# mLSTM heads on one core: scores from stacked key and query parts, row picks over 128 rows, partition sums from split operands

## The chip, the cores and the metric

One of the eight cores of a Trainium2 chip runs the whole program. The metric is the device time in microseconds; the kernel before has a median of 2092.24 us over 3 runs (2091.16 to 2093.17).

## The reference, cut to what matters

A two-layer decoder trunk, 512 tokens of width 1024, in float32: feed-forward (`ffn0`), mLSTM mixer, `ffn1`, shared keys and values (`kv`), `ffn2`, sparse attention (`nsa`), `ffn3`. Each feed-forward block is `h += 0.5 * (silu(a) * b) @ w_out` with `a, b = split(rmsnorm(h) @ w_in)`. The mLSTM has 8 heads (keys and queries of 64, values of 128). Per head, with all times before `t` in one causal triangle:

```
log_i, log_f = gate projections;  b = cumsum(log_f)
D[t,s] = b[t] - b[s] + log_i[s]   (s <= t);   m[t] = max over s
W[t,s] = exp(D[t,s] - m[t]) * (q[t] . k[s]) / 8
num[t] = sum_s W[t,s] v[s];   den[t] = sum_s W[t,s]
h_out  = rmsnorm(num / max(|den|, exp(-m))) * gain * sigmoid(og)
```

## The kernel before, in words

Everything is kept transposed: features on the 128 partitions, the 512 tokens along the free dimension. A float32 product of full accuracy is made from three matmuls of the type float32r: each operand is split into a rounded part `hi` (ScalarE, L152 or L124) and a rest `lo` (VectorE, L153 or L125), and `mm3` (L145) adds `hi*hi + hi*lo + lo*hi` in PSUM. All matmuls go through `mm` (L142), so the profile puts them on L143; they are told apart by tile names.

Weights come through `load_weight` (L105): a DMA on the SP queue into `wraw` (2 buffers), a split into `whi` and `wlo` (3 buffers each), two weights ahead of use. A plain float32 operand is accepted by TensorE too; the profile then shows two matmul instructions for one in the code.

The mLSTM stage (`mlstm`, L312) runs in this order (L534 to L551):

- the gate projection `pg` (40 of 128 output rows; PSUM tag `mm`, which has two buffers), then the query projection of the first pair of heads; then `rstd_rows` (the row scale `r`) and `gates` (L347), a chain of some 20 VectorE operations on 8 rows, which ends in the running maximum. Its rows are transposed (`um`, L379) and split by `pair` (L331) into `nM`, a tile of 40 rows: the `hi` rows at 0 to 7, the `lo` rows at 32 to 39.
- `project_qk` (L386) and `project_v` (L404) of four heads (half 0). Queries and keys of two heads share a tile of 128 rows, 64 rows each, as `qkh` and `qkl`.
- `heads(0)` (L447), woven with the output-gate projection `og`, 1.5 steps of it for each step of the heads. Per head: the decay matrix `E` for the next head (`decay`, L432; a row pick `sel[:, h, :]` of 40 rows spreads row `h` of `nM` over all partitions: tile `pnm`); the scores `S` in four causal strips of 512, 384, 256 and 128 columns, each an `mm3` over the head's 64 rows (L459); the product with `E` on VectorE (L466), its split `Wh`, `Wl`; the sum over strips on GpSimd (L469); the product with the values (`pn`, L477), its copy `num` and square `sqn` on ScalarE; and two plain float32 matmuls into the 40 rows of `dm` (L484, L485), which sum `E` and `sqn` over the partitions. The stationary operand is a slice of `hot`, all zeros but one column, so that the sum lands in the head's row.
- projections of half 1, woven with `finish(0)` (L490): a copy of `dm`, transposes, a short VectorE chain, and per head a row pick of `cr` (L513), two elementwise steps and a split into `yhi`, `ylo`. Then `heads(1)` woven with the output projection `out0` at 0.4, `finish(1)` woven with the rest of it, and the output projection of half 1.

A scheduler under this code orders the instructions of each engine by readiness and the order of the code, so engines' orders differ a little from what is written. Each feed-forward stage opens a pool of its own (L260); its first tile, `home` (L262), has a size that depends on the stage, 384, 128, 256 and 448 bytes for stages 0 to 3, and the tiles `ft`, `fu`, `ghi` and `glo` lie behind it. The pools of `ffn2` and `ffn3` begin behind the tiles of `kv` (L561 to L566), whose sizes add up to 37,376 bytes, 73 times 512.

Of the kernel before, what the change touches and what calls it, by code (L numbers as in the profile page):

```python
# [9 lines left out]
F32 = mybir.dt.float32  # L10
F32R = mybir.dt.float32r
# [14 lines left out]
THIRDS = ((0, 8), (8, 15), (15, 22))  # L26
HOME = (0, 256, 384, 64)
H = 8
# [62 lines left out]
class Net:  # L91
# [164 lines left out]
    def ffn(self, i, r=None):  # L256
        nc, tc = self.nc, self.tc
        with ExitStack() as ctx:
            pp = ctx.enter_context(tc.tile_pool(name=f"fps{i}", bufs=6, space=PSUM, reuse_waits="tile"))
            gp = ctx.enter_context(tc.tile_pool(name=f"fg{i}", bufs=8, reuse_waits="tile"))  # L260

            nc.vector.memset(gp.tile([P, (HOME[i] - 128) % 512 // 4], F32, name="home", tag="home", bufs=1)[:, :1], 0.0)  # L262
            x, ssq = self.norm_in(G_FFN + i * KB, r is None, i == 0)
# [48 lines left out]
    def mlstm(self):  # L312
        nc, tc = self.nc, self.tc
        TT, STT, TS = nc.vector.tensor_tensor, nc.vector.scalar_tensor_tensor, nc.vector.tensor_scalar
        with ExitStack() as ctx:
# [7 lines left out]

            sel = mp.tile([40, H, P], F32R, name="sel")
            nc.gpsimd.tensor_copy(sel, self.cst[:40, C_SEL:C_SEL + H][:, :, None].to_broadcast([40, H, P]))

            hot = mp.tile([P, 80], F32, name="hot")
            nc.gpsimd.memset(hot, 0.0)
            nc.gpsimd.memset(hot[:, 39:40], 1.0)

            def pair(name, src):  # L331

                t = mp.tile([40, T], F32R, name=name, tag="rows", bufs=2)
                nc.gpsimd.memset(t.bitcast(F32), 0.0)
                nc.scalar.activation(t[:H], src, AF.Copy)
                TT(t[32:], src, t[:H].bitcast(F32), op=ALU.subtract)
                return t


            w = self.weight("m_gate")  # L340
            pg = ps_mm()
            for k in range(KB):
# [43 lines left out]
            def project_qk(half):  # L386
                for j in range(2):
                    for kind in range(2):
                        w = self.weight("m_qk", 4 * kind + 2 * half + j)
                        ps = ps_mm()  # L390
                        for k in range(KB):
                            self.mm3(ps, self.strip(w, k), x[k], k == 0, k == KB - 1)
                            yield
                        s = mp.tile([P, T], F32, name="qks", tag="tmp", bufs=3)
                        if kind == 0:
                            STT(s, ps, 0.125, r, op0=ALU.mult, op1=ALU.mult)
                        else:
                            TT(s, ps, r, op=ALU.mult)
                        hi = mp.tile([P, T], F32R, name="qkh", tag="qk", bufs=8)
                        lo = mp.tile([P, T], F32R, name="qkl", tag="qk", bufs=8)  # L400
                        self.split(s, hi, lo)
                        qk[kind, 2 * half + j] = (hi, lo)

# [28 lines left out]
            def decay(h):  # L432

                nm = ps_nm()
                self.mm(nm, sel[:, h, :], nM, True, True)
                E = mp.tile([P, 1280], F32, name="E", tag="big", bufs=BIG)
                dg = mp.tile([P, NTB, P], F32, name="dg", tag="tmp", bufs=3)
                for sb in range(NTB):
                    u = uc[:, sb, h:h + 1]
                    STT(dg[:, sb, :], nm[:, sb * P:(sb + 1) * P], u, self.cst[:, C_CAUST:C_CAUST + P], op0=ALU.add, op1=ALU.add)  # L440
                    if sb < NTB - 1:
                        nc.scalar.activation(E[:, SEG[sb] + P:SEG[sb] + T - sb * P], nm[:, (sb + 1) * P:], AF.Exp, bias=u)
                for sb in range(NTB):
                    nc.scalar.activation(E[:, SEG[sb]:SEG[sb] + P], dg[:, sb, :], AF.Exp)
                return E

            def heads(half):  # L447
                first = 4 * half
                E = decay(first)
                d = dm[half] = pp.tile([40, T], F32, name="dm", tag="dm", bufs=1)  # L450
                for h in range(first, first + 4):
                    base = 64 * (h % 2)
                    pick = lambda t, a, b: (t[0][base:base + 64, a:b], t[1][base:base + 64, a:b])
                    q, k = qk[0, h // 2], qk[1, h // 2]
                    S = [pp.tile([P, T], F32, name="S", tag="S", bufs=3) for _ in range(3)]
                    for sb in (0, 1, 3, 2):
                        bank, c0 = BANK[sb]
                        n = T - sb * P
                        self.mm3(S[bank][:, c0:c0 + n], pick(k, sb * P, sb * P + P), pick(q, sb * P, T), True, True)  # L459
                        yield  # L460
# [22 lines left out]
                    yield  # L483
                    self.mm(d, hot[:, 39 - h:79 - h], E[:, :T], h == first, False)  # L484
                    self.mm(d, hot[:, 7 - h:47 - h], sq, False, h == first + 3)  # L485
                    num[h] = n
# [3 lines left out]
            def finish(half):  # L490

                d = dm[half]
                s = mp.tile([40, T], F32, name="ds", tag="tmp", bufs=3)
                nc.scalar.copy(s, d)
                pt = ps_nm()[:, :160].rearrange("p (t c) -> p t c", t=NTB)
# [15 lines left out]
                for h in range(4 * half, 4 * half + 4):  # L511
                    pc = ps_nm()
                    self.mm(pc, sel[:, h, :], cr, True, True)  # L513
                    n = num[h]
# [554 lines left out]
```

## Time and profile before

| | us |
|---|---|
| median of 3 runs | 2092.24 |
| the profiled execution, its own time | 2092.58 |
| its span, first to last instruction | 2090.8 |
| TensorE busy in the span | 2058.5 (98%) |
| mean granted TensorE clock | 0.998 |

The span is 1.8 us shorter than the execution's own time, which is the start and the end of the program. The matmuls overlap in the trace: one of 512 columns shows 390 ns, but the next starts some 227 ns after it. So costs on TensorE are read from start to start. "Idle before" in brackets is the time in which an engine had nothing running, with what ended it.

### The profile page before, as it was taken

The numbers are of one execution on the slowest core, as the hardware profiler recorded it, in microseconds if no ns is written. First come the engines' busy times: TensorE is split into PE (matmuls) and PEld (weight loads), VectorE is DVE, ScalarE is ACT, GpSimd is POOL, SyncE is SP. The second block draws the span as 40 slices with busy tenths as digits, with TensorE's granted clock in tenths as the row PEclk, the third lists the DMA queues.
The fourth block names the chain that finished last, engine by engine and source line by source line (L and its number), as shares of the span: only waits on it lengthen the run. The fifth ranks groups of instructions, "written<-read, shape, count | busy, mean of one in ns | idle before, by whom it ended". The sixth has DMA issues, their size and how long they took to land.

```text
span 2090.8 us, 24459 instructions
## 1 busy us (share of the span) xinstructions
PE 2058.5 (98%) x9492; PEld 1663.3 (80%) x9492; DVE 1144.4 (55%) x2020; ACT 767.4 (37%) x1269; POOL 160.4 (8%) x174
## 2 busy tenths in 40 slices
PE   8999999999999999999999999999999999999999
PEld 6888888767668888888877888888778788888887
DVE  6434445754765434445666444445899985434443
ACT  5222233344543223224343322224667663222231
POOL 1000001001220000000101000001343310000000
PEclk9999999999999999999999999999999999999999
DMA  4323332212112332323324323332121112232232
GB/s 158 93 99 99 95 100 87 88 61 71 61 59 90 94 101 90 102 94 97 111 91 124 108 95 95 97 97 88 51 61 41 36 57 91 92 100 96 96 99 93
DMA packets 55188, 186.02 MB, mean 89 GB/s; under 512 B 6560, under 2 KB 7200, under 8 KB 55072
## 3 DMA queue, kind: packets, MB, share of 16 engines
q1 hardware_dynamic: 54112, 182.37, 27.4%
q8 instruction: 74, 1.21, 0.2%
q0 software_dynamic: 384, 1.05, 0.2%
q10 hardware_dynamic: 576, 1.05, 0.1%
q14 instruction: 42, 0.34, 0.1%
HBM read 177.10 MB, written 2.10 MB: 86 GB/s over the span
## 4 chain that ended last, share of the span: by engine, by line
PE 92%; DVE 5%; ACT 1%; issue 1%; POOL 0%; DMA 0%; SPq 0%; ACTq 0%; DVEq 0%; POOLq 0%
PE pmm L143 81%; PE S L143 3%; PE po L143 2%; PE vps L143 1%; PE pt L862 1%; PE paux L143 1%; PE dm L143 1%; DVE wlo L125 1%; PE pn L143 1%; DVE pr L828 1%; DVE ptl L153 0%; DVE qh L745 0%; DVE Wl L153 0%; ACT xhi L187 0%; PE pnm L143 0%
## 5 line engine op out<-in xcount | busy, mean ns | idle before, releaser
L124 ACT ACTIVATE whi<-wraw 128x1024 fp32r<-128x1024 f32 (+4 forms) x399 | 359.8, 916 | 1023.4 <-PE pmm L143 838.2
L143 PE MATMUL pmm<-xhi,whi 128*128 128x512 f32 (+1 forms) x1680 | 664.5, 396 | 10.8 <-ACT whi L124 8.5
L143 PE MATMUL pmm<-xhi,wlo 128*128 128x512 f32 (+1 forms) x1680 | 658.6, 392 | 0.0
L143 PE MATMUL pmm<-xlo,whi 128*128 128x512 f32 (+1 forms) x1680 | 658.4, 392 | 0.0
L125 DVE TENSOR_TENSOR wlo<-wraw,whi 128x1024 fp32r<-128x1024 f32 (+4 forms) x399 | 421.8, 1068 | 82.3 <-ACT whi L124 71.7
L143 PEld LDWEIGHTS pmm<-xhi,whi 128*128 128x128 f32 (+1 forms) x1680 | 316.0, 188 | 82.1 <-ACT whi L124 9.7
L143 PEld LDWEIGHTS pmm<-xhi,wlo 128*128 128x128 f32 (+1 forms) x1680 | 315.6, 188 | 67.7 <-DVE wlo L125 1.1
L143 PEld LDWEIGHTS pmm<-xlo,whi 128*128 128x128 f32 (+1 forms) x1680 | 316.0, 188 | 62.4
L143 PE MATMUL pmm<-ghi,whi 128*128 128x512 f32 x704 | 276.1, 392 | 0.0
L143 PE MATMUL pmm<-ghi,wlo 128*128 128x512 f32 x704 | 275.7, 392 | 0.0
L143 PE MATMUL pmm<-glo,whi 128*128 128x512 f32 x704 | 275.1, 391 | 0.0
L271 DVE TENSOR_TENSOR fu<-pmm,r 128x512 f32<-128x512 f32 x88 | 60.8, 691 | 260.6 <-PE pmm L143 260.4
L309 DVE SCALAR_TENSOR_TENSOR h<-pmm,h 128x512 f32<-128x512 f32 x96 | 66.3, 691 | 250.6 <-PE pmm L143 250.6
L269 DVE TENSOR_TENSOR ft<-pmm,r 128x512 f32<-128x512 f32 x88 | 60.8, 691 | 174.8 <-PE pmm L143 174.8
L143 PEld LDWEIGHTS pmm<-ghi,wlo 128*128 128x128 f32 x704 | 132.2, 188 | 29.4
L143 PEld LDWEIGHTS pmm<-glo,whi 128*128 128x128 f32 x704 | 132.2, 188 | 29.1
L143 PEld LDWEIGHTS pmm<-ghi,whi 128*128 128x128 f32 x704 | 132.3, 188 | 28.2
L198 POOL TENSOR_TENSOR ssq<-ssq,sq 128x512 f32<-128x512 f32 x18 | 27.3, 1518 | 1024.2 <-ACT sq L197 1024.2
L152 ACT ACTIVATE ghi<-ft 128x512 fp32r<-128x512 f32 x88 | 55.7, 632 | 72.6 <-DVE ft L272 72.6
L829 ACT ACTIVATE pr<-pr,nx 128x512 f32<-128x512 f32 (+3 forms) x128 | 70.7, 555 | 8.6 <-DVE pr L828 7.9
L153 DVE TENSOR_TENSOR glo<-ft,ghi 128x512 fp32r<-128x512 f32 x88 | 60.4, 686 | 14.7 <-ACT ghi L152 14.7
L828 DVE TENSOR_SCALAR_CACHE_REDUCE pr<-S,cn 128x512 f32<-128x512 f32 (+3 forms) x128 | 66.1, 537 | 2.7 <-PE S L143 2.5
(289 smaller groups left out, 2037.5 us busy)
## 6 DMA issues: line engine op xcount, KB each, us to landing
wraw<-in_ffn_in SPq DMA_DIRECT2D x176, 512.0 KB, 3.4
wraw<-in_ffn_out SPq DMA_DIRECT2D x64, 448.0 KB, 3.4
wraw<-in_ffn_out SPq DMA_DIRECT2D x32, 512.0 KB, 3.5
wraw<-in_m_qk SPq DMA_DIRECT2D x8, 512.0 KB, 3.4
wraw<-in_m_v SPq DMA_DIRECT2D x8, 512.0 KB, 3.4
wraw<-in_m_og SPq DMA_DIRECT2D x8, 512.0 KB, 3.4
wraw<-in_m_out SPq DMA_DIRECT2D x8, 512.0 KB, 3.4
wraw<-in_kv_t SPq DMA_DIRECT2D x8, 512.0 KB, 3.5
```

Of the source, the lines that this page charges most:

```text
L124: nc.scalar.activation(hi[:p, c], raw[:p, c], AF.Copy)
L125: nc.vector.tensor_tensor(lo[:p, c], raw[:p, c], hi[:p, c].bitcast(F32), op=ALU.subtract)
L143: self.nc.tensor.matmul(out, lhsT, rhs, start=start, stop=stop)
L152: self.nc.scalar.activation(hi, src, AF.Copy)
L153: self.nc.vector.tensor_tensor(lo, src, hi.bitcast(F32), op=ALU.subtract)
L198: (nc.gpsimd if b < 4 else nc.vector).tensor_tensor(t, t, sq, op=ALU.add)
L269: nc.vector.tensor_tensor(t, pa, r, op=ALU.mult)
L271: nc.vector.tensor_tensor(u, pb, r, op=ALU.mult)
L309: nc.vector.scalar_tensor_tensor(h, po[j], 0.5, h, op0=ALU.mult, op1=ALU.add)
L828: TS(s, S[:, i, :n], cc, None, op0=ALU.mult, op1=ALU.min, accum_out=nx[:, i:i + 1])
L829: nc.scalar.activation(s, s, AF.Exp, bias=nx[:, i:i + 1], scale=-1.0, accum_out=z[:, i:i + 1])
L862: nc.tensor.transpose(pt[:, col:col + P], pr[br][:, ROW[tb] + sb * P:ROW[tb] + sb * P + P], self.ident)
```

## The change

- **Scores.** The keys of a head become one tile of 128 rows, `hi` on 64 rows and `lo` on the other 64; the queries of a head become two tiles, `hi` and `lo`, each held on both halves, the second by a DMA inside SBUF on the SP queue. A strip is then two matmuls over 128 rows in place of three over 64. The splits are made per head (64 rows) and no longer per pair.
- **Row picks.** `nM` and `cr` have 128 rows, zeros outside the 16 used, and `sel` is one column for each head, broadcast to 128 columns. `sel` and `hot` are written by ScalarE in place of GpSimd.
- **Partition sums.** `dm` has 128 rows. `E` and the square are split into `hi` and `lo` (ScalarE and VectorE) in tiles of the pool `stat`, and each sum is two float32r matmuls with 128 stationary columns.
- `pg` moves from PSUM tag `mm` (2 buffers) to tag `S` (3 buffers).
- `home` has 384 bytes in every feed-forward stage.

```diff
-            nc.vector.memset(gp.tile([P, (HOME[i] - 128) % 512 // 4], F32, name="home", tag="home", bufs=1)[:, :1], 0.0)
+            nc.vector.memset(gp.tile([P, 96], F32, name="home", tag="home", bufs=1)[:, :1], 0.0)
...
-            sel = mp.tile([40, H, P], F32R, name="sel")
-            nc.gpsimd.tensor_copy(sel, self.cst[:40, C_SEL:C_SEL + H][:, :, None].to_broadcast([40, H, P]))
-
-            hot = mp.tile([P, 80], F32, name="hot")
-            nc.gpsimd.memset(hot, 0.0)
-            nc.gpsimd.memset(hot[:, 39:40], 1.0)
+            sel = mp.tile([P, H], F32R, name="sel")
+            nc.scalar.activation(sel, self.cst[:, C_SEL:C_SEL + H], AF.Copy)
+            pick = lambda h: sel[:, h:h + 1].to_broadcast([P, P])
+
+            hot = mp.tile([P, 168], F32R, name="hot")
+            nc.scalar.activation(hot, self.cst[:, C_ID:C_ID + 1].to_broadcast([P, 168]), AF.Copy, scale=0.0)
+            nc.scalar.activation(hot[:, 39:40], self.ones[:, :1], AF.Copy)
...
-                t = mp.tile([40, T], F32R, name=name, tag="rows", bufs=2)
+                t = mp.tile([P, T], F32R, name=name, tag="rows", bufs=2)
...
-            pg = ps_mm()
+            pg = pp.tile([P, T], F32, name="pg", tag="S", bufs=3)
...
-                        hi = mp.tile([P, T], F32R, name="qkh", tag="qk", bufs=8)
-                        lo = mp.tile([P, T], F32R, name="qkl", tag="qk", bufs=8)
-                        self.split(s, hi, lo)
-                        qk[kind, 2 * half + j] = (hi, lo)
+                        for e in range(2):
+                            a, b = slice(64 * e, 64 * e + 64), slice(64 - 64 * e, 128 - 64 * e)
+                            if kind == 0:
+                                hi, lo = (mp.tile([P, T], F32R, name=n, tag="q", bufs=8) for n in ("qh", "ql"))
+                                self.split(s[a], hi[a], lo[a])
+                                for t in (hi, lo):
+                                    nc.sync.dma_start(t[b].bitcast(F32), t[a].bitcast(F32))
+                                qk[0, 4 * half + 2 * j + e] = (hi, lo)
+                            else:
+                                t = mp.tile([P, T], F32R, name="kk", tag="k", bufs=4)
+                                self.split(s[a], t[a], t[b])
+                                qk[1, 4 * half + 2 * j + e] = t
...
-                self.mm(nm, sel[:, h, :], nM, True, True)
+                self.mm(nm, pick(h), nM, True, True)
...
-                d = dm[half] = pp.tile([40, T], F32, name="dm", tag="dm", bufs=1)
+                d = dm[half] = pp.tile([P, T], F32, name="dm", tag="dm", bufs=1)
+                def total(row, src, last, *tags):
+                    hi, lo = (self.sp.tile([P, T], F32R, name=n, tag=t, bufs=k) for n, (t, k) in zip(("th", "tl"), tags))
+                    self.split(src, hi, lo)
+                    for t in (hi, lo):
+                        self.mm(d, hot[:, 39 - row:167 - row], t, row == first and t is hi, last and t is lo)
...
-                        self.mm3(S[bank][:, c0:c0 + n], pick(k, sb * P, sb * P + P), pick(q, sb * P, T), True, True)
+                        for part in range(2):
+                            self.mm(S[bank][:, c0:c0 + n], k[:, sb * P:sb * P + P], q[part][:, sb * P:], part == 0, part == 1)
...
-                    self.mm(d, hot[:, 39 - h:79 - h], E[:, :T], h == first, False)
-                    self.mm(d, hot[:, 7 - h:47 - h], sq, False, h == first + 3)
+                    total(h, E[:, :T], False, ("ssq0", 1), ("ssq1", 1))
+                    total(32 + h, sq, h == first + 3, ("sq", 2), ("sq", 2))
```

## Rows read from the trace of the kernel before

**Rows 1.** The page, busy time of the engines: us, share of span, instructions.

```profile
PE 2058.5 (98%) x9492; PEld 1663.3 (80%) x9492; DVE 1144.4 (55%) x2020; ACT 767.4 (37%) x1269; POOL 160.4 (8%) x174
```

**Rows 2.** The page, the chain that ended last, by line.

```profile
PE pmm L143 81%; PE S L143 3%; PE po L143 2%; PE vps L143 1%; PE pt L862 1%; PE paux L143 1%; PE dm L143 1%; DVE wlo L125 1%; PE pn L143 1%; DVE pr L828 1%; DVE ptl L153 0%; DVE qh L745 0%; DVE Wl L153 0%; ACT xhi L187 0%; PE pnm L143 0%
```

**Rows 3.** Windows of the mLSTM: us, then each engine's busy us (instructions), PEclk.

```profile
378.00:405.40 27.40, 25.12 (x110) 20.70 (x110) 21.84 (x42) 8.43 (x14) 0.00 (x0) 0.94 0.17 58
...
428.00:506.00 78.00, 76.92 (x311) 50.83 (x310) 39.18 (x66) 31.37 (x69) 10.47 (x12) 1.00 0.17 55
...
553.00:596.00 43.00, 42.41 (x173) 25.92 (x172) 29.37 (x52) 24.84 (x57) 10.78 (x12) 1.00 0.12 39
```

**Rows 4.** Timeline of PE in heads(0): start, us; scores of one strip.

```profile
487.79 0.40 PE L143 MATMUL pmm<-xhi,wlo 128*128 128x512 f32 x1
488.12 0.49 PE L143 MATMUL S<-qkh 64*128 64x512 f32 x1
...
489.35 0.39 PE L143 MATMUL pmm<-xlo,whi 128*128 128x512 f32 x1
```

**Rows 5.** Timeline of PE in heads(0): partition sums of one head.

```profile
503.56 0.40 PE L143 MATMUL pmm<-xhi,wlo 128*128 128x512 f32 x1
503.89 1.05 PE L143 MATMUL dm<-E,hot 128*40 128x512 f32 x2
...
506.06 0.39 PE L143 MATMUL pmm<-xlo,whi 128*128 128x512 f32 x1
```

**Rows 6.** Timeline of PE in heads(0): a row pick between its two neighbours.

```profile
435.73 0.39 PE L143 MATMUL pmm<-xhi,wlo 128*128 128x512 f32 x1
...
436.82 0.39 PE L143 MATMUL pmm<-xlo,whi 128*128 128x512 f32 x1
```

**Rows 7.** Timeline of PE in heads(1): three strips in one run.

```profile
553.87 0.39 PE L143 MATMUL S<-qkh 64*128 64x512 f32 x1
...
555.44 0.50 PE L143 MATMUL pmm<-yhi,whi 128*128 128x512 f32 x1
```

**Rows 8.** Groups by form: splits in heads and projections; busy us, mean ns.

```profile
L153 DVE TENSOR_TENSOR Wl<-E,Wh 128x512 fp32r<-128x512 f32 x16 | 14.5, 919 | 2.5 <-ACT Wh L152 2.5
...
L152 ACT ACTIVATE Wh<-E 128x512 fp32r<-128x512 f32 x16 | 9.8, 625 | 10.0 <-DVE E L466 10.0
...
L153 DVE TENSOR_TENSOR qkl<-qks,qkh 128x512 fp32r<-128x512 f32 x8 | 5.4, 680 | 0.0
```

**Rows 9.** Timeline of DVE in heads(1): a subtract while POOL sums.

```profile
564.26 1.39 DVE L153 TENSOR_TENSOR Wl<-E,Wh 128x512 fp32r<-128x512 f32 x1
```

**Rows 10.** The chain in order of time, heads(0): a wait on a split.

```profile
439.65 1.54 DVE Wl L153
```

**Rows 11.** Timeline of PE, end of finish(1): idle and its releaser in brackets.

```profile
611.94 0.51 PE L143 MATMUL pmm<-yhi,whi 128*128 128x512 f32 x1 [0.57 <-ACT yhi L152]
```

**Rows 12.** Timeline of PE after the row scale: the wait, then slow steps.

```profile
387.33 0.50 PE L143 MATMUL pmm<-xhi,whi 128*128 128x512 f32 x1 [2.28 <-DVE f L352]
...
388.01 0.63 PE L143 MATMUL pmm<-xhi,wlo 128*128 128x512 f32 x1
388.44 0.63 PE L143 MATMUL pmm<-xhi,whi 128*128 128x512 f32 x1
```

**Rows 13.** Timeline of PE in project_v(0): transposes of the gate rows.

```profile
415.02 0.41 PE L379 MATMUL pnm<-cst,um 40*128 40x40 f32 x4 [0.38 <-DVE um L374]
```

**Rows 14.** The chain in four 35 us stretches: start, us, matmuls; ffn0, ffn2 (two), ffn3.

```profile
334.86 35.36 PE pmm L143 x156
...
1239.91 35.13 PE pmm L143 x155
...
1417.85 35.23 PE pmm L143 x151
...
2049.00 35.02 PE pmm L143 x153
```

**Rows 15.** DMA issues: KB each, median us from issue to landing.

```profile
qh<-qh SPq DMA_DIRECT2D x16, 128.0 KB, 2.3
```

More of the change, by code (lines that the diff above doesn't have):

```diff
@@ L26 @@
 THIRDS = ((0, 8), (8, 15), (15, 22))
-HOME = (0, 256, 384, 64)
 H = 8
@@ L321, in mlstm @@
             x, ssq = self.norm_in(G_MIX)
-            sel = mp.tile([40, H, P], F32R, name="sel")
-            nc.gpsimd.tensor_copy(sel, self.cst[:40, C_SEL:C_SEL + H][:, :, None].to_broadcast([40, H, P]))
-            hot = mp.tile([P, 80], F32, name="hot")
-            nc.gpsimd.memset(hot, 0.0)
-            nc.gpsimd.memset(hot[:, 39:40], 1.0)
+            sel = mp.tile([P, H], F32R, name="sel")
[4 more added lines that the diff above has]
+            nc.scalar.activation(hot[:, 39:40], self.ones[:, :1], AF.Copy)
             def pair(name, src):
-                t = mp.tile([40, T], F32R, name=name, tag="rows", bufs=2)
+                t = mp.tile([P, T], F32R, name=name, tag="rows", bufs=2)
                 nc.gpsimd.memset(t.bitcast(F32), 0.0)
                 nc.scalar.activation(t[:H], src, AF.Copy)
-                TT(t[32:], src, t[:H].bitcast(F32), op=ALU.subtract)
+                TT(t[32:32 + H], src, t[:H].bitcast(F32), op=ALU.subtract)
                 return t
             w = self.weight("m_gate")
-            pg = ps_mm()
+            pg = pp.tile([P, T], F32, name="pg", tag="S", bufs=3)
             for k in range(KB):
@@ L449, in heads @@
                 E = decay(first)
-                d = dm[half] = pp.tile([40, T], F32, name="dm", tag="dm", bufs=1)
+                d = dm[half] = pp.tile([P, T], F32, name="dm", tag="dm", bufs=1)
[4 more added lines that the diff above has]
+                        self.mm(d, hot[:, 39 - row:167 - row], t, row == first and t is hi, last and t is lo)
                 for h in range(first, first + 4):
-                    base = 64 * (h % 2)
-                    pick = lambda t, a, b: (t[0][base:base + 64, a:b], t[1][base:base + 64, a:b])
-                    q, k = qk[0, h // 2], qk[1, h // 2]
+                    q, k = qk[0, h], qk[1, h]
                     S = [pp.tile([P, T], F32, name="S", tag="S", bufs=3) for _ in range(3)]
@@ L493, in finish @@
                 s = mp.tile([40, T], F32, name="ds", tag="tmp", bufs=3)
-                nc.scalar.copy(s, d)
+                nc.scalar.copy(s, d[:40])
                 pt = ps_nm()[:, :160].rearrange("p (t c) -> p t c", t=NTB)
@@ L512, in finish @@
                     pc = ps_nm()
-                    self.mm(pc, sel[:, h, :], cr, True, True)
+                    self.mm(pc, pick(h), cr, True, True)
                     n = num[h]
```

## The prediction, made before the changed kernel ran

> **What bounds the kernel now.** The page first: TensorE is busy for 98% of the span [rows 1], and the chain that ended last lies almost wholly on its lines [rows 2]; the parts that the change rewrites, S, dm and pnm, have some 4% there. So what shortens the order of matmuls shortens the kernel, until another engine is late. Next the windows of the mLSTM [rows 3]: in heads(0) VectorE has 39.2 us to do in 78, in heads(1) 29.4 in 43. The second has little room, the first much. The first window shows a granted clock of 0.94 where all others have 1.00. Last the timeline of TensorE, start to start. An ordinary step of 512 columns takes 35.36 / 156 = 0.227 us [rows 14], and by that every other step is judged.
>
> **Scores.** A plain matmul, three score matmuls of 64 rows and the next plain one take 487.79 to 489.35, 1.56 us [rows 4], where five ordinary steps take 1.13. So a strip between matmuls of 128 rows pays a toll of 0.43 us over its three steps, half of it going in (the next matmul starts 0.33 us after the last, not 0.23), half coming out. The change leaves two passes, with 128 rows like their neighbours. Removed per head: one pass over 1280 columns, 2.5 x 0.227 = 0.57, and four tolls, 1.72; 2.29 us. In heads(1) strips often stand together (three strips in 553.87 to 555.44, 1.57 us [rows 7], within 0.1 of ordinary steps), so I count two to three tolls and 1.6 us a head.
>
> **Partition sums.** Four dm matmuls and two neighbours take 503.56 to 506.06, 2.50 us [rows 5]; less two ordinary steps, 2.05. Four float32r steps make 0.91. Saved: 1.14 a head.
>
> **Row picks.** One with its neighbours takes 435.73 to 436.82, 1.09 [rows 6]; less two steps 0.64, afterwards 0.23. Saved: 0.41, eight times in the heads (0.25 in heads(1), where some stand by S), and eight times in the finishes.
>
> **What this is worth by stage.** heads(0): 4 x (2.29 + 1.14 + 0.41) = 15.4 us of TensorE. New on the other engines: two splits a head. A subtract on VectorE is 0.68 us in the projections and 0.92 in the heads [rows 8], 1.39 in the row that GpSimd's sum runs beside [rows 9]; a copy on ScalarE 0.63 [rows 8]. Eight subtracts of 0.68 to 1.39 are 5.4 to 11 us, so VectorE comes to 45 to 50 in some 63 us: TensorE still sets this stage. But waits such as 1.54 us for Wl [rows 10] grow when the matmuls ahead of them are shorter; I take back 2.4 and keep **13**.
> heads(1): 4 x (1.6 + 1.14 + 0.25) = 12 us of TensorE, to 31; VectorE goes to 35 to 40. So here VectorE becomes the bound: 37.5 us, a gain of 5.5 rather than 12. Behind it finish(1) waits for the last sum, whose square now needs a copy and a subtract first, 0.63 + 0.68 = 1.3 later. Its own four picks (1.6) bring nothing: TensorE already runs out of work there, 0.57 us idle for yhi [rows 11]. Kept: **4**, with 0 and 12 as ends.
> finish(0) lies under value projections that TensorE does without a pause: 4 x 0.41, **1.6**.
>
> **The gate projection's buffer.** After the row scale TensorE idles 2.28 us, ended by f on L352 [rows 12]. That operation reads pg; the key projection needs the `mm` buffer that pg holds. With pg under `S` a buffer is free, and the scores' buffers are first needed by the value projection, three projections later. After the idle the steps are 0.43 us [rows 12], the lower of the clock's two levels; the window's 0.94 makes 0.06 x 27.4 = 1.6 us [rows 3]. Together 3.9. What is late next: the gate chain on VectorE starts at the same time as before and gets four more subtracts (four projections, one split more each, 2.7 us), while TensorE arrives earlier. The transposes already waited 0.38 us for its end [rows 13]; placed as before they would wait up to 6 us more, put behind more value matmuls nothing. heads(0) begins at 428 [rows 3], 13 us after those transposes. I take back 1.5 and keep **2.4**, ends -2 and 3.9.
>
> **The address of ghi and glo.** The same matmuls with moving ghi or glo step by 0.2267 in ffn0 (35.36 / 156), 0.2333 in ffn2 (35.23 / 151) and 0.2289 in ffn3 (35.02 / 153); the x matmuls of ffn2 step by 0.2266 (35.13 / 155) [rows 14]. So it isn't the stage, but the tile. What differs is `home`: 384, 256 and 448 bytes, on bases that are a multiple of 512 apart. With 384 everywhere, ffn2 and ffn3 get ffn0's place modulo 512. Each has 528 such matmuls (22 blocks x 8 outputs x 3): 528 x 0.0066 = 3.5 and 528 x 0.0022 = 1.2, **4.7** us. ffn1 keeps its step, since it has 384 too now. The mLSTM's own tiles move as well, by a few ns on some 250 matmuls; under 1 us either way, taken as nothing.
> The Trainium skill speaks against this part: SBUF — State Buffer, section SBUF: two separate sides, lets only VectorE and GpSimd contend and says that TensorE never waits on anyone, and names no cost of a start address. By it the sum would be 4.7 us smaller; the rows of one instruction at three speeds stand against it, though no run before the change moved the tile alone.
>
> **Costed at nothing.** The 16 query copies stand on SP's queue among the weight loads and wait there for a split; the like copies of the attention land in 2.3 us [rows 15], and the heads need them a value projection later, 96 steps or 22 us. Weights are two ahead, 2 x 24 steps or 11 us, which covers an SP held for 2 us; if that cover went, each copy would hold the next weight by up to 2.3 us. The projections' splits go from 8 to 16, each as long with 64 rows as with 128, since the columns are the same: 8 x 0.68 = 5.4 us more on VectorE [rows 8], under 2 x 96 steps or 44 us of matmuls. `sel` and `hot` on ScalarE: three small copies in a stretch where it is busy 8.4 of 27 us [rows 3]. The GpSimd fills of 128 rows go along the same 512 columns.
>
> **Sum.** 13 + 4 + 1.6 + 2.4 + 4.7 = 25.7 us off the profiled execution's 2092.58 is 2066.9; the median lies 0.34 lower, so **2066.5**.
>
> **The rivals.**
> *TensorE's whole cut arrives.* The scheduler fills heads(1) with output projection and finds room for the gate chain: 15.4 + 12 + 3.2 + 3.9 + 4.7 = 39 less, 2053. For it: TensorE's share; against it: VectorE's 29.4 of 43. Chance 0.14.
> *Half of it is lost.* heads(1) and the gate stretch give nothing and heads(0) loses 4 more to waits for splits: 2066.5 + 4 + 2.4 + 4 = 2077. For it: VectorE's load and the wait in rows 10. Chance 0.2.
> *The address does nothing*, so that the change doesn't do what `home` seems made for: 2066.5 + 4.7 = 2071. For it: other things could differ by stage; against it: ffn2's x matmuls. Chance 0.09. This is what the Trainium skill's page cited above would have.
> *Slower: the sums stand in TensorE's queue ahead of work that is ready.* In place of plain matmuls on data at hand, dm then waits for num, square, copy and subtract, 0.6 + 0.6 + 0.63 + 0.92 = 2.8 us, and with GpSimd in the way 3.2. If nothing stands between pn and dm in the queue, 8 x 3.2 = 26, and the clock falls after each pause as in rows 12, 8 x 1.6 = 13; 39 in all, 2105. The point of decision is a loss of 25.7 / 8 = 3.2 us a head. Against it: before, some plain matmuls stand between them in heads(0). Chance 0.04.
> *No difference*: gains and waits cancel; 0.03.
>
> **How the numbers follow.** The forecast has 0.5. Its own spread is some 6 us; the range takes it, the address case, most of the full cut and the halved one: 2055 to 2077. A difference under 0.2% (4.2 us) can't be told from none here. Faster 0.93, same 0.03, slower 0.04.
>
> **What would show it.** S steps of 0.227, 0.17, 0.12 and 0.11 with ordinary neighbours; two matmuls each for E and the square at 0.227; no 2.28 us idle after the row scale and a clock of 1.00 in that window; ghi steps of 0.2267 in ffn2 and ffn3; VectorE over 90% busy in heads(1). Wrong would be: new idle before dm ended by a split, a wait of several us before the um transposes, or steps of 0.43 in the heads.

## The result, and the profile after

The changed kernel takes **2070.48 us** in the median of 4 runs (2067.81 to 2072.25), the kernel before 2092.34 beside it: a ratio of 0.9895, 95% interval 0.9878 to 0.9912, 21.9 us less. The profiled execution is the longest of the four, 2072.25 us with a span of 2070.5, 20.3 us less than the profiled one of before.

The page of the kernel after, busy time and the chain by line:

```profile
PE 2032.7 (98%) x9460; PEld 1666.6 (80%) x9460; DVE 1155.9 (56%) x2044; ACT 782.3 (38%) x1296; POOL 161.1 (8%) x171
...
PE pmm L142 79%; PE S L142 3%; PE po L142 2%; PE pt L879 1%; PE vps L142 1%; PE paux L142 1%; DVE wlo L124 1%; POOL E L486 1%; DVE qh L762 0%; DVE pr L845 0%; DVE rq L219 0%; DVE ptl L152 0%; PE dm L142 0%; ACT xhi L186 0%; DVE Wl L152 0%
```

TensorE is 25.8 us less busy than in [rows 1], 5.5 us more than the time has fallen: part of what its order lost came back as idle time. Two names in this list are not in [rows 2]: `rq` at 0%, and at 1% `POOL E L486`, GpSimd's sum over the strips, for which TensorE waited only 0.2 us in heads(1) before.

To find the place, the mLSTM is cut at matmuls that both traces have: the first column sum of the row scale, the first row pick (heads(0) begins), the first transpose of `ds` (finish(0)), the first matmul with `yhi` (about where heads(1) begins), the second transposes of `ds` (finish(1)), and the last matmul with `yhi`. The five windows between them, first in the kernel before, then in the kernel after (us; busy us of PE, PEld, DVE, ACT, POOL with their instructions; granted clock; DMA share; GB/s):

```profile
377.70:428.30 50.60, 47.94 (x214) 39.10 (x212) 36.70 (x64) 16.72 (x29) 0.00 (x0) 0.97 0.26 83
428.30:530.50 102.20, 101.12 (x418) 70.78 (x417) 50.15 (x84) 42.33 (x89) 10.47 (x12) 1.00 0.19 62
530.50:555.40 24.90, 24.73 (x107) 18.28 (x106) 18.07 (x35) 10.25 (x18) 5.96 (x5) 1.00 0.26 85
555.40:596.40 41.00, 40.41 (x164) 24.11 (x162) 27.29 (x49) 23.10 (x55) 10.78 (x12) 1.00 0.11 37
596.40:632.90 36.50, 35.54 (x150) 26.32 (x149) 27.83 (x50) 16.20 (x27) 9.95 (x7) 1.00 0.23 76
```

```profile
377.60:429.10 51.50, 49.02 (x213) 40.26 (x212) 39.87 (x68) 19.63 (x33) 0.00 (x0) 0.93 0.34 103
429.10:518.50 89.40, 87.98 (x401) 70.90 (x399) 57.64 (x96) 49.64 (x101) 10.49 (x12) 1.00 0.27 83
518.50:541.20 22.70, 22.48 (x104) 18.17 (x104) 17.36 (x35) 9.31 (x17) 5.95 (x5) 1.00 0.27 89
541.20:580.40 39.20, 34.93 (x159) 27.41 (x157) 32.62 (x59) 27.94 (x64) 11.26 (x12) 0.96 0.13 43
580.40:617.50 37.10, 33.81 (x140) 25.85 (x140) 27.24 (x49) 16.32 (x27) 10.70 (x7) 0.95 0.21 70
```

heads(0) is 12.8 us shorter and TensorE is as full there as before (87.98 of 89.40). heads(1) is only 1.8 shorter: TensorE has 5.5 us less to do and 4.3 us idle, where it had 0.6. The early stage is 0.9 us longer and finish(1) 0.6. The clock, 1.00 in all of heads(1) and finish(1) before, is 0.96 and 0.95.

Now TensorE's own timeline in the kernel after: a strip of scores and one head's sums in heads(0); the gate rows' transposes; and the middle of heads(1) (start, us, what; in brackets the idle time before and what ended it):

```profile
480.62 0.39 PE L142 MATMUL pmm<-xhi,wlo 128*128 128x512 f32 x1
480.84 0.33 PE L142 MATMUL S<-qh,kk 128*128 128x384 f32 x1
481.01 0.34 PE L142 MATMUL S<-ql,kk 128*128 128x384 f32 x1
481.19 0.39 PE L142 MATMUL pmm<-xhi,whi 128*128 128x512 f32 x1
...
492.56 0.40 PE L142 MATMUL dm<-th,hot 128*128 128x512 f32 x1
492.79 0.39 PE L142 MATMUL dm<-tl,hot 128*128 128x512 f32 x1
493.02 0.39 PE L142 MATMUL dm<-th,hot 128*128 128x512 f32 x1
493.36 0.50 PE L142 MATMUL dm<-tl,hot 128*128 128x512 f32 x1
493.70 0.40 PE L142 MATMUL pmm<-xhi,whi 128*128 128x512 f32 x1
...
412.77 0.39 PE L142 MATMUL vps<-whi,xhi 128*128 128x512 f32 x1
415.64 0.61 PE L379 MATMUL pnm<-cst,um 40*128 40x40 f32 x4 [2.48 <-DVE um L374]
...
417.20 0.63 PE L142 MATMUL vps<-whi,xhi 128*128 128x512 f32 x1
417.63 0.63 PE L142 MATMUL vps<-wlo,xhi 128*128 128x512 f32 x1
...
559.27 0.28 PE L142 MATMUL pn<-Wh,vl 128*128 128x256 f32 x1
561.15 0.50 PE L142 MATMUL dm<-th,hot 128*128 128x512 f32 x1 [1.61 <-ACT th L151]
...
562.70 0.63 PE L142 MATMUL pmm<-yhi,whi 128*128 128x512 f32 x1
563.12 0.63 PE L142 MATMUL pmm<-ylo,whi 128*128 128x512 f32 x1
```

The strip of 384 columns has two steps of 0.17 and a neighbour of 0.22: no toll, unlike [rows 4]. (Each of the two passes carries two of the four products of parts, so `lo*lo`, which the three passes left out, is now in the sum as well.) The sums of `E` take two ordinary steps, those of the square two of 0.34, 1.14 us in all where [rows 5] gave 2.05. The transposes wait 2.48 us (0.38 in [rows 13]), from start to start 2.87, and behind them come 12 steps of 0.427, the clock's lower level. In heads(1) `dm` waits for `th`, 1.89 us from start to start, and 7 slow steps follow.

The waits of heads(1) in the kernel after (us in total, times, longest):

```profile
ACT th L151 <- POOL E L486: 5.8, 4, 2.0
PEld dm L142 <- ACT th L151: 5.5, 5, 1.8
PE dm L142 <- ACT th L151: 4.0, 4, 1.6
```

Read upwards: TensorE waits for the copy to `th`, and the copy for GpSimd's sum. In heads(0), where 1.5 steps of `og` stand by each step of the heads and not 0.4 of `out0`, the same chain cost TensorE nearly nothing: it waits 0.2 us for a `tl` there and never for a `th`.

The feed-forward stages, by the chain in four stretches of 35 us (ffn0, two in ffn2, ffn3), as in [rows 14]:

```profile
335.90 35.13 PE pmm L142 x155
...
1220.94 35.13 PE pmm L142 x155
...
1398.88 35.13 PE pmm L142 x155
...
2024.96 35.13 PE pmm L142 x155
```

All four now step by 35.13 / 155 = 0.2266; the third was 0.2333 and the fourth 0.2289.

### The profile page after: what moved, and what is told of

Read it like the earlier page. It is cut to its first block, busy times and chain, and to the rows that moved or that the text cites. A ratio compares the mean times of both kernels' runs of the same rounds, so it can differ in the third digit from the quotient of the medians.

```text
span 2070.5 us, 24480 instructions
## 1 busy us (share of the span) xinstructions
PE 2032.7 (98%) x9460; PEld 1666.6 (80%) x9460; DVE 1155.9 (56%) x2044; ACT 782.3 (38%) x1296; POOL 161.1 (8%) x171
## 4 chain that ended last, share of the span: by engine, by line
PE 89%; DVE 6%; ACT 2%; issue 1%; POOL 1%; DMA 0%; SPq 0%; ACTq 0%; DVEq 0%; POOLq 0%
PE pmm L142 79%; PE S L142 3%; PE po L142 2%; PE pt L879 1%; PE vps L142 1%; PE paux L142 1%; DVE wlo L124 1%; POOL E L486 1%; DVE qh L762 0%; DVE pr L845 0%; DVE rq L219 0%; DVE ptl L152 0%; PE dm L142 0%; ACT xhi L186 0%; DVE Wl L152 0%
## 5 line engine op out<-in xcount | busy, mean ns | idle before, releaser
L142 PE MATMUL pmm<-xhi,whi 128*128 128x512 f32 x1672 | 657.6, 393 | 7.7 <-ACT whi L123 7.7
L142 PE MATMUL pmm<-xlo,whi 128*128 128x512 f32 x1672 | 653.9, 391 | 0.0
L142 PE MATMUL pmm<-xhi,wlo 128*128 128x512 f32 x1672 | 653.8, 391 | 0.0
L142 PEld LDWEIGHTS pmm<-xhi,whi 128*128 128x128 f32 x1672 | 314.5, 188 | 70.6 <-ACT whi L123 8.9
L142 PEld LDWEIGHTS pmm<-xhi,wlo 128*128 128x128 f32 x1672 | 314.3, 188 | 66.8 <-DVE wlo L124 1.1
L142 PEld LDWEIGHTS pmm<-xlo,whi 128*128 128x128 f32 x1672 | 314.6, 188 | 61.8
```

What stands on the lines that cost most here:

```text
L142: self.nc.tensor.matmul(out, lhsT, rhs, start=start, stop=stop)
```

## The experiments

All stage lengths come from one profiled execution each, cut as above; "ffn2" is the stretch that holds it, from the first column sums of `kv` to those of the sparse attention, and "ffn3" the one from the last matmul of the attention's output projection to the end of the program. The cuts are read to 0.1 us, so a length can be 0.1 off. In us:

| kernel | early | heads(0) | finish(0) | heads(1) | finish(1) | ffn2 | ffn3 | median |
|---|---|---|---|---|---|---|---|---|
| before | 50.6 | 102.2 | 24.9 | 41.0 | 36.5 | 460.4 | 366.7 | 2092.34 |
| before + home | 50.6 | 102.2 | 25.0 | 41.0 | 36.5 | 456.8 | 365.3 | 2086.61 |
| before + pg in S | 47.3 | 102.1 | 25.0 | 40.9 | 36.6 | 460.3 | 366.7 | 2087.93 |
| before + scores | 50.8 | 94.1 | 24.7 | 37.6 | 36.5 | 459.4 | 366.7 | 2081.36 |
| before + sums, picks | 50.5 | 97.9 | 23.4 | 42.0 | 36.8 | 459.5 | 366.7 | 2086.6 |
| after | 51.5 | 89.4 | 22.7 | 39.2 | 37.1 | 457.3 | 365.4 | 2070.48 |
| after, pg back | 50.7 | 89.4 | 22.6 | 40.4 | 37.5 | 455.8 | 365.3 | 2072.32 |
| after, old home | 51.5 | 89.4 | 22.6 | 39.3 | 37.1 | 460.9 | 366.7 | 2075.2 |
| after, plain sums | 50.2 | 91.3 | 22.6 | 37.1 | 35.9 | 456.8 | 365.3 | 2068.33 |
| after, um late | 48.0 | 89.4 | 22.6 | 40.3 | 37.2 | 458.2 | 365.3 | 2067.23 |
| after, direct sums | 50.2 | 89.4 | 22.6 | 34.8 | 35.9 | 457.1 | 365.3 | 2063.44 |
| both of these | 48.0 | 89.4 | 22.6 | 34.8 | 35.8 | 456.2 | 365.3 | 2061.88 |

Three bounds for reading it. The ffn2 stretch differs by 2.4 us between kernels with the same feed-forward code (455.8 to 458.2). heads(1) differs by 1.2 us between four kernels with the same code there: 39.2, 39.3, 40.3 and 40.4 (after, old home, um late, pg back). The early stage of the kernel after comes out as 51.5 or as 50.2 with the same code ("plain sums" and "direct sums" don't touch it): the wait for `um` is 2.9 us from start to start in all of them, but 12 slow steps follow it in one case and 7 in the other, 5 x 0.2 = 1.0 us. The profiled executions of after, old home and um late are the longest of their runs.

### One part of the change at a time, on the kernel before

**The address alone.**

```diff
-gp.tile([P, (HOME[i] - 128) % 512 // 4], F32, name="home", tag="home", bufs=1)
+gp.tile([P, 96], F32, name="home", tag="home", bufs=1)
```

> The kernel before with 384 bytes of home in every feed-forward stage and nothing else. Theory (the place of ghi and glo sets their step): 4.7 us less than before, about 2087.6, with ghi steps of 0.227 us in ffn2 and ffn3. Rival (the steps belong to the stage): no difference, 2092.3, and steps of 0.233 and 0.229 as before.

Measured 2086.61 against 2092.45, ratio 0.9970 (0.9959 to 0.9982): 5.8 us less. ffn2 gives 3.6 and ffn3 1.4. Only the tiles of the feed-forward pools moved, and the steps that changed are those of the matmuls that read `ghi` and `glo`, so it is the place of these tiles. Not every move matters: in ffn1 `home` grew from 128 to 384 bytes, and the `ghi` steps there are 0.2267 us in both kernels. The Trainium skill, SBUF — State Buffer, section SBUF: two separate sides, says that only VectorE and GpSimd share a port and that TensorE never waits on anyone, and it names no cost of a start address; the steps of 0.2333 and 0.2267 for the same matmul disagree with reading it as if any place were as good as another. Why one place is slower, no run here shows.

**The buffer of the gate projection alone.**

```diff
-            pg = ps_mm()
+            pg = pp.tile([P, T], F32, name="pg", tag="S", bufs=3)
```

> The kernel before with only pg moved to the scores' buffers. Theory (the gate chain on VectorE is what ends last): the idle of 2.28 us after the row scale goes and comes back at the transposes of the gate rows, with slow steps behind it; heads(0) begins at 428 to 429 us as before, and the time is within 1.5 us of before. Rival (the buffer was the limit): heads(0) begins 3.9 us earlier, about 2088.4.

Measured 2087.93, ratio 0.9977 (0.9967 to 0.9987): 4.5 us less, 3.3 of them in the early stage. The wait did not merely move. The waits of TensorE in that stage:

```profile
PE pnm L379 <- DVE um L374: 1.2, 1, 1.2
```

The 2.28 us of [rows 12] are replaced by 1.2, and no slow step follows. The gate chain has gained too: in its course VectorE idled 1.00 us for ScalarE and 0.36 and 0.55 for key and query products that TensorE's pause had delayed, now 0.29 in all; from `f` to the end of `um` it takes 26.5 us in place of 28.3. Another 0.7 us of the gain lies at the start of ffn1, where TensorE waits 0.84 us for a weight's copy and not 1.52. It does so in every kernel with `pg` under `S`; why is not shown.

**The scores alone** (the picks keep their 40 rows, with `sel` as one broadcast column).

```diff
-                        self.mm3(S[bank][:, c0:c0 + n], pick(k, sb * P, sb * P + P), pick(q, sb * P, T), True, True)
+                        for part in range(2):
+                            self.mm(S[bank][:, c0:c0 + n], k[:, sb * P:sb * P + P], q[part][:, sb * P:], part == 0, part == 1)
```

> The kernel before with only the scores from stacked parts (row picks read one column of sel, still 40 rows; sums as before). Theory (one pass and four tolls of 0.43 us a head, all on the path in heads(0)): heads(0) 9 us shorter, heads(1) 3 to 6 us shorter, together 2077 to 2081. Rival (a head is held by the other engines): under 4 us less, 2088 or more.

Measured 2081.36, ratio 0.9945 (0.9932 to 0.9957): 11.1 us less; heads(0) 8.1, heads(1) 3.4.

**The sums and the row picks alone** (the diff's hunks for `sel`, `hot`, `pair`, `dm`, `total` and the two picks).

```diff
-                    self.mm(d, hot[:, 39 - h:79 - h], E[:, :T], h == first, False)
-                    self.mm(d, hot[:, 7 - h:47 - h], sq, False, h == first + 3)
+                    total(h, E[:, :T], False, ("ssq0", 1), ("ssq1", 1))
+                    total(32 + h, sq, h == first + 3, ("sq", 2), ("sq", 2))
```

> The kernel before, with the row picks by 128 rows and the partition sums by split operands alone; scores, the gate projection's buffer and home as before. Theory: in heads(0) they give what the scores did not, 89.4 against 94.1 us of the kernel with the scores alone, so some 4.7 us (102.2 to 97.5); in heads(1) the sums cost about what they save, because dm waits there for th behind GpSimd's sum (41.0 stays 40 to 42); the finishes give 1 to 2. So 2092.0 less 5 to 6.5: 2085.5 to 2087. Rival A, from the sum of the parts: the home edit, the buffer and the scores alone gave 5.8, 4.5 and 11.1, together 21.4 of the whole's 21.9, so sums and picks give nothing: 2091 to 2092. Rival B, by the forecast's own terms with nothing lost: 8 x 1.14 and 16 x 0.41 are 15.7: 2076.

Measured 2086.6, ratio 0.9976 (0.9968 to 0.9985): 5.1 us less, near the slow end of the theory's 2085.5 to 2087. heads(0) gives 4.3 and finish(0) 1.5, while heads(1) is 1.0 us *longer*. Rival A, that they give nothing, falls, and so does rival B's 2076. So the parts give 5.8 + 4.5 + 11.1 + 5.1 = 26.5 us one by one and 21.9 together; 4.6 us are lost where they meet. The intervals of these medians are 4 to 7 us wide each, so alone they would not settle it, but the stages of the table say the same, and where: early, the parts change the stage by -3.3, +0.2 and -0.1, the whole by +0.9, 4.1 lost; in heads(1) by -0.1, -3.4 and +1.0, the whole by -1.8, 0.7 lost.

### Undoing one part in the kernel after

**The buffer back.**

```diff
-            pg = pp.tile([P, T], F32, name="pg", tag="S", bufs=3)
+            pg = ps_mm()
```

> The changed kernel with pg back in the two-buffer tag. Theory (the gate chain ends last in either case): heads(0) begins within 1.5 us of 429 us, time 2069 to 2072. Rival (moving pg paid and something else ate it): 3.9 us slower, about 2074.4.

Measured 2072.32, ratio 0.9904 (0.9891 to 0.9918): 1.8 us slower than after by the medians, with overlapping intervals. The early stage has its 2.2 us wait for `f` back and is not longer for it, 50.7. What is worth 4.5 us alone is worth 1.8 by the medians here, and nothing in the early stage. From `f` to the end of `um` VectorE takes 28.9 us, as in the kernel with the scores alone (28.9) and in after (29.0).

**The old home.**

```diff
-gp.tile([P, 96], F32, name="home", tag="home", bufs=1)
+gp.tile([P, (HOME[i] - 128) % 512 // 4], F32, name="home", tag="home", bufs=1)
```

> The kernel after, with the old sizes of home (384, 256 and 448 bytes by stage) and nothing else. Theory: the address is a matter of ffn2 and ffn3 alone, apart from the mLSTM, so undoing it costs what those two stages gained from before to after, 3.1 + 1.3 = 4.4 us, up to the 5.8 us that it gave alone: 2075 to 2076.5. Rival: part of the 5.8 us was the place of the mLSTM's or the first stage's tiles, which is shifted in another way in this kernel: 2072 to 2074.

Measured 2075.2, ratio 0.9920 (0.9907 to 0.9934): 4.7 us slower than after, as the theory has it. The chain in the stretches of ffn2 and ffn3 that rows 14 show, in this kernel:

```profile
1398.80 35.39 PE pmm L143 x152
...
2024.88 35.19 PE pmm L143 x154
```

0.2328 and 0.2285: the slow steps are back, in the same two stages.

### What the changed kernel waits for

**The sums as plain float32 again**, with 128 output rows and no split.

```diff
-                    hi, lo = (self.sp.tile([P, T], F32R, name=n, tag=t, bufs=k) for n, (t, k) in zip(("th", "tl"), tags))
-                    self.split(src, hi, lo)
-                    for t in (hi, lo):
-                        self.mm(d, hot[:, 39 - row:167 - row], t, row == first and t is hi, last and t is lo)
+                    self.mm(d, hot[:, 39 - row:167 - row], src, row == first, last)
```

> The kernel after, with the partition sums of E and of the square again as one plain float32 matmul of the source itself, 128 columns of output, no th and tl. Theory: in heads(1) the sums by split operands cost more in waits than their steps save, since the trace of after shows TensorE idle 1.9 us twice and 0.7 us twice ahead of dm there, ended by the copy to th behind GpSimd's sum of E; in heads(0) they save 1.14 us a head on TensorE. So heads(0), from the first row pick to the transposes of ds, goes from 89.4 to some 94 us, heads(1), from the first yhi matmul to the second transposes of ds, from 39.2 to 36 to 38, and the time is 2069 to 2073. Rival A: the split sums are worth their steps in both halves, 8 x 1.14 = 9 us: 2079. Rival B: they are worth nothing even in heads(0), since VectorE there holds the matmuls back: heads(0) stays within 1 us of 89.4 and the time is 2066 to 2068.

Measured 2068.33, ratio 0.9885 (0.9867 to 0.9903), not told apart from after. heads(0) is 1.9 us longer, not 4.6; heads(1) is 2.1 and finish(1) 1.2 shorter. So the split of the sums pays in the first half, and costs more in the second, 3.3 us by these executions; heads(1)'s 37.1 lies below all four lengths given above for the code of after. GpSimd's sum still holds TensorE here, 1.6 us ahead of one `dm`. The step of 1.14 us a head can be taken apart: in this kernel's timeline the four float32 passes of a head begin 0.429 us apart, 1.72 in all, where 40 output rows took 2.05 [rows 5]. 0.33 us is thus the toll of the 40 rows, and the split itself saves 1.72 less 1.14, 0.58.

**The transposes of the gate rows later.**

```diff
-            nM, uc, e2 = gates()
+            nM, um = gates()
             run(qk0)
-            run(project_v(0))
+            pv = project_v(0)
+            for _ in range(26):
+                next(pv)
+            uc, e2 = gate_columns(um)
+            run(pv)
```

> The kernel after, with the transposes of the gate rows um, and what follows from them, emitted behind 26 of the 32 steps of the value projection in place of ahead of it. Theory: the 2.48 us that TensorE waits for um in the trace of after, and the dozen steps at 0.427 us that follow (12 x 0.2 = 2.4 us), go, because value matmuls that are ready fill that time: 4 to 5 us less, heads(0) begins at 424 to 425 us, and the time is 2066. Rival: the start of heads(0) is set by the chain of the gates on VectorE and not by TensorE, so that the wait only moves to the first row pick or to the first Wh: heads(0) begins no earlier than 428 us or its first steps wait, and the time stays 2070 to 2071.

Measured 2067.23, ratio 0.9882 (0.9867 to 0.9898): 3.3 us less than after by the medians (the intervals overlap); the early stage goes from 51.5 to 48.0. What TensorE waits for there now, in its timeline:

```profile
414.46 0.50 PE L142 MATMUL vps<-wlo,xhi 128*128 128x512 f32 x1 [1.71 <-DVE wlo L124]
```

The wait for `um` is gone; in its place the next weight's split is late, since it stands on VectorE behind gate operations and key splits. But that pause is 2.1 us and not 2.9 from start to start, and no slow step follows it: 0.8 + 12 x 0.2 = 3.2 of the 3.5 us. The theory named the right place; its cure brought 3.3 of the 4 to 5 us that it gave.

**heads(1)'s sums of E straight from the strips.**

```diff
-                    for sb in range(1, NTB):
+                    for sb in range(1, NTB) if half == 0 else ():
...
-                    total(h, E[:, :T], False, ("ssq0", 1), ("ssq1", 1))
+                    if half == 0:
+                        total(h, E[:, :T], False, ("ssq0", 1), ("ssq1", 1))
+                    else:
+                        for sb in order:
+                            for t in (hi, lo):
+                                self.mm(d[:, sb * P:], hot[:, 39 - h:167 - h], t[:, strips[sb]], h == first and sb == 0 and t is hi, False)
```

> The kernel after, with heads(1)'s sums of E taken by matmuls straight from the strips of Wh and Wl, two parts of four strips, in place of GpSimd's sum of the strips and its split into th and tl. Per head TensorE gets 2.5 x 2 = 5 steps' worth of columns for E in place of 2. Theory: heads(1) is held by the chain VectorE subtract, GpSimd sum, copy to th, dm: with the sum and the copy away, the waits ahead of dm (1.9, 1.9, 0.8 and 0.7 us) and the slow steps behind the first go: heads(1) from 39.2 us to 36 to 37.5, the time 2067 to 2069. Rival A: VectorE's own work, 34 of 40 us, sets heads(1): its end moves by under 1 us, and the time is 2070. Rival B: the added columns, 4 x 3 x 0.227 = 2.7 us of TensorE, stand on the path and nothing goes: 2073.

Measured 2063.44, ratio 0.9862 (0.9846 to 0.9878): 7.0 us less than after. heads(1) takes 34.8 us, beyond what the theory gave, and finish(1) 1.2 less; 1.3 of the rest is the early stage's varying clock. Its window:

```profile
539.60:574.40 34.80, 34.01 (x176) 27.91 (x174) 26.28 (x54) 25.95 (x60) 0.00 (x0) 1.00 0.15 51
```

TensorE has *more* to do, 176 matmuls against 159 in the window, and is full; rivals A and B both fall. VectorE is 6.3 us less busy (32.62 to 26.28). 2.8 of that are the four `tl` of `E`; another part shows in the groups of VectorE, in heads(1) of after and then of this kernel:

```profile
L152 DVE TENSOR_TENSOR Wl<-E,Wh 128x512 fp32r<-128x512 f32 (+1 forms) x12 | 9.0, 771 | 0.2 <-ACT Wh L151 0.2
...
L124 DVE TENSOR_TENSOR wlo<-wraw,whi 128x512 fp32r<-128x512 f32 x6 | 5.4, 905 | 0.0
```

```profile
L152 DVE TENSOR_TENSOR Wl<-E,Wh 128x512 fp32r<-128x512 f32 (+1 forms) x12 | 7.0, 598 | 1.1 <-ACT Wh L151 1.1
...
L124 DVE TENSOR_TENSOR wlo<-wraw,whi 128x512 fp32r<-128x512 f32 x6 | 3.9, 683 | 0.0
```

The same twelve subtracts cost 771 ns beside GpSimd's sums and 598 without them, the weights' 905 and 683: 3.5 us. The Trainium skill's page SBUF — State Buffer, section SBUF: two separate sides, has this as the one place of contention among the engines, a VectorE operation with two SBUF inputs against a GpSimd one that reads SBUF; the rows agree. How much of the gain is the shorter chain and how much VectorE's relief was not taken apart. The plain sums, which keep GpSimd's sum and drop `th` and `tl`, gave 2.1 of the 4.4 us in heads(1).

**Both edits.**

> The two edits together on the kernel after: the transposes of um behind 26 steps of the value projection, and heads(1)'s sums of E straight from Wh and Wl. Theory: they lie in different stretches, so their effects add: 2070.5 less 4.5 less 2.5 is 2063.5, range 2061 to 2066. Rival: both waits only move, 2069 to 2071.

Measured 2061.88 (2061.27 to 2062.39), ratio 0.9853 (0.9836 to 0.9871). The stages add, 48.0 and 34.8, at a clock of 1.000 over the span. This version beats both kernels, and its interval lies below that of after. The theory's sum was 1.6 us higher.

**And finish(1)'s products on VectorE.**

```diff
-                    nc.gpsimd.tensor_tensor(n, n, sig[h], op=ALU.mult)
+                    (nc.gpsimd if half == 0 else nc.vector).tensor_tensor(n, n, sig[h], op=ALU.mult)
```

> The kernel with both edits (um late, heads(1)'s sums direct), and with finish(1)'s products by sig on VectorE in place of GpSimd. Theory: finish(1) waits for yhi behind GpSimd's product, 1.37 us each beside about 0.7 us for such a tile on VectorE; the waits of 1.1, 0.9 and 0.2 us in the output projection go: 1 to 3 us less than 2061.9, 2059 to 2061. Rival: VectorE has h and the weight splits in that stretch, the product queues behind them, and the time is the same or 1 us longer, 2062 to 2063.

Measured 2062.31, ratio 0.9863 (0.9849 to 0.9876): no gain; finish(1) takes 35.7 us in place of 35.8. The rival held: each product takes 0.68 us on VectorE in place of 1.37 and brings nothing there. This says nothing on the change.

## Why the prediction was right, and where not

Forecast 2066.5, measured 2070.5. The sign, most of the size and the largest terms came out; two of the smaller terms failed, both by a wait that the forecast had named. Together these two were 6.4 of its 25.7 us and came to 0.3.

**heads(0): right, 13 against 12.8**, but not by its own account. The scores alone gave 8.1 where 4 x 2.29 = 9.2 stood, sums and picks 4.3 where 4 x 1.55 = 6.2 stood. So TensorE's steps saved 12.4 and not 15.4, and the 2.4 us set aside for waits on splits were not needed: `pn` waits 1.1 us for `Wl` in the stage before and after. (The 1.54 us of [rows 10] are the time that the chain spent in that subtract; TensorE's own wait behind it was 0.58.) Two steps were too large. The toll of 0.43 was read at one strip and taken for all sixteen: 8.1 us less the four passes' 2.3 leave 0.36 a strip. And `dm`'s four steps come to 1.14 us, not 0.91, since those of the square take 0.34 each. With 1.14 the sums and picks would give 5.3; the last 1.0 us down to 4.3 stays open. The errors cancelled: that 13 met 12.8 is luck.

**heads(1) and finish(1): wrong, 4 against 1.2.** The step that failed is "here VectorE becomes the bound". VectorE is busy for 32.6 of 39.2 us, 83% and not over 90%. What TensorE waits for is the chain GpSimd's sum, copy to `th`, `dm`, with the matmuls behind `dm` held in TensorE's queue: the mechanism of the rival "slower", which was costed for all eight heads and acted in heads(1) only. The row of [rows 9] showed GpSimd's sum at work there, but its price as a wait went into the rival alone and was left out of the forecast. With the chain cut, heads(1) falls by 6.2 us against before, near the 5.5 that the forecast had for it, with VectorE at 75% (26.28 of 34.80). That edit also relieved VectorE, so the two are not separated. finish(1)'s end was foreseen 1.3 us later for the square's split. It is 1.2 us longer in after than with the plain or the direct sums, but the direct sums keep the square's split, so this isn't its cause. In after TensorE waits 2.1 us for `yhi` there, with plain sums 0.8; why `yhi` is later was not looked into.

**finish(0): 1.6 against 2.2**, right in the main; the sums and picks alone gave 1.5.

**The gate projection's buffer: wrong, 2.4 against a loss of 0.9** (a gain of 0.4 where 7 slow steps follow and not 12). The idle 2.28 and the slow steps behind it are gone, as foreseen: the window of [rows 3] has a clock of 1.00 and TensorE without a gap,

```profile
378.00:405.40 27.40, 27.40 (x128) 22.92 (x128) 23.15 (x44) 10.39 (x17) 0.00 (x0) 1.00 0.29 85
```

but all of it comes back at the `um` transposes. The forecast saw that they "would wait up to 6 us more, put behind more value matmuls nothing", and took 1.5 us for it, a value between the two with no row behind it; the outcome lies on the side of its end of -2. That 1.5 is the step that failed. The buffer alone, 3.3 us in this stage, shows that the pause is not a fixed length that merely moves. What eats it is another part of the change, the splits of queries and keys by 64 rows. `f` and the end of the gate chain on VectorE, with the buffer alone and then in after:

```profile
386.11 0.68 DVE L352 TENSOR_TENSOR f<-pg,r 8x512 f32<-8x512 f32 x1
...
411.95 0.68 DVE L374 TENSOR_TENSOR um<-t,t 8x512 f32<-8x512 f32 x1
```

```profile
386.45 0.68 DVE L352 TENSOR_TENSOR f<-pg,r 8x512 f32<-8x512 f32 x1
...
414.81 0.68 DVE L374 TENSOR_TENSOR um<-t,t 8x512 f32<-8x512 f32 x1
```

From `f` to the end of `um` it takes 26.5 and then 29.0 us, and `um` ends at 412.6 and then at 415.5, with no idle over 0.3 us in either. In after VectorE does eight of these splits in between (four `ql` and four `kk`, 5.5 us), with the buffer alone four (2.6), and two weight splits fewer (1.3 us). That makes 1.6 of the 2.5 us; the rest lies between the operations. The kernel with the scores alone, which has the new splits and not the buffer, takes 28.9 too. The forecast had named the four more subtracts in the gate chain, 2.7 us, close to these 2.5, but did not subtract them, nor the earlier arrival of TensorE, in full. Its other account of the same splits, under "costed at nothing" with a cover of 44 us of TensorE, was right about the matmuls and wrong about the gates, which share VectorE with them.

**The address: right, 4.7.** Undone in the changed kernel it costs 4.7 by the medians; alone it gave 5.8, of which the two stages show 5.0; the rest is within the noise. The rival that it does nothing falls. The steps are 0.2266 in all stages, the one thing the forecast had down to the number.

**Costed at nothing, and so it was**: the query copies (no matmul waits for `qh` or `ql`), `sel` and `hot`.

Of what should have shown it wrong, all three appeared, each in one place: idle ahead of `dm` ended by a split (heads(1)), a wait of 2.5 us before the `um` transposes, and steps of 0.43 in the heads. By the profiled executions the terms came to 12.8 + 2.2 + 1.2 - 0.9 + 4.4 = 19.7 of 20.3 us, in place of 25.7; the rest is the 0.7 us at the start of ffn1.

## What to carry to other kernels

Here a matmul over 64 rows, or onto 40, between full ones cost more than its own columns (0.36 us a strip, 0.33 a head's sums), so stacked parts and padded rows paid where TensorE set the time. A step that is moved to cheaper matmuls by splitting its operand puts a copy and a subtract ahead of the queue: ask, stage by stage, how many ready matmuls stand between it and its source, and where there are few, sum the parts that are already split. And cost two edits together wherever both load the same engine: in the early stage the buffer alone gave 3.3 us, the scores with their new splits lost 0.2, and the whole change lost 0.9.

## What was not expected of the hardware

- The same float32r matmul steps by 226.7, 229.0 or 233.3 ns by the place of its moving tile alone (means over the `ghi` and `glo` steps of a stage, with `home` of 384, 448 and 256 bytes; in ffn1 128 bytes give 226.7 as well).
- After a pause of about 2.9 us from start to start ahead of the `um` transposes, 12 slow steps follow in two kernels and 7 in two others, with the same matmuls up to there; after four pauses of 1.6 to 2.1 us in that stage none. In heads(1) four kernels have two pauses of 1.89 us each, and in each of the four no slow step follows one of them and 7 or 8 follow the other. So a pause's price in clock, 0 to 2.4 us here, can be nearly as large as the pause, and varies between executions; the runs of the kernel after spread over 4.4 us, those of the version with both edits, whose clock is 1.000, over 1.1.
- A plain float32 matmul of 512 columns onto 128 rows takes two passes of 0.429 us, against two float32r passes of 0.227 behind a split. In this kernel the split paid in heads(0), where matmuls stood ready, and not in heads(1).
